# Projection results in ring tiles, two to a tile, with an aligned layout and an earlier split, in a hybrid decoder layer on one core

## The chip, the cores and the metric

The kernel runs on one core of a Trainium2 chip. The metric is device time in microseconds of one execution. TensorE (PE in the profile, with its weight loads as PEld) multiplies, VectorE (DVE) and ScalarE (ACT) do elementwise work and copy results out of PSUM, the queue of SyncE (SP) loads weights and stores results, and the queue of GpSimd (POOL) loads and stores the mixer's data. Each engine takes its instructions in the order in which a scheduler has put them when the program is built.

## The reference

One layer over 2048 rows of width 1024, in float32:

```python
mod = cond @ w_ada + b_ada                      # six vectors: shift, scale, gate, twice
h = modulated_rmsnorm(x, norm_mix, shift1, scale1)
z = h @ w_in                                    # split in 14 pieces
mixed = concatenate([gla_group(...), hgrn2_group(...), mlstm_group(...)])
x = x + gate1 * (mixed @ w_out)
h = modulated_rmsnorm(x, norm_mlp, shift2, scale2)
ff = square(relu(h @ w_ff1)) @ w_ff2            # 1024 -> 4096 -> 1024
x = x + gate2 * ff
return rms(x) * final_norm
```

The three groups are chunkwise linear attentions of different kinds with 64-wide heads. They carry a state along the sequence.

## The kernel before

The sequence is cut in four quarters of 512 rows. A float32 operand of a large matmul is split in a high part (a cast to float32r, on ScalarE, line 193) and a low part (what is left, on VectorE, line 194). Each product is three matmuls: high by high, high by low, low by high.

**Stage 1, the projections** (`inproj`, lines 771 to 878). The four quarters run one after the other. The columns of `w_in` form nine groups, in the order f, q, conv, hout, gout, m, gqk, hi, gv. A group has four row tiles of 128, each in a PSUM bank of its own, and its weights come in four parts (`part`), so the four banks are complete one after the other at the group's end. `evac` then copies each bank out, with the function that the group needs, into a buffer `st`, of which there are three, and stores it to DRAM; a buffer is free when its store has landed. `conv` uses `st` as well, and the two tags `st` and `cvr` also serve the gate step `gla_gate`. The normalized and modulated input of a quarter is eight tiles `ht` of a ring of 15 (`ring`, line 212), a tile being a high and a low half of 512 columns. The tiles of the next quarter are made by `h_k` (lines 224 to 226: VectorE, ScalarE, VectorE), which the program emits in the last group.

**Mixer work in the background.** `mix` and `block_pass` compute the attentions of a quarter from what stage 1 has stored. The program emits their pieces between large matmuls, by `pump`, which keeps a budget against due times; `finish(q)` emits what is left of quarter q. `prog.hold` keeps a new quarter of `mix` from starting while its buffers are lent out.

**Stage 2** per quarter: the output projection (`outproj_in` loads the mixed rows into lent mixer buffers, called spare, and splits them into ring tiles; `outproj` multiplies them and adds x), the norm (`rstd`, with the matmul `ps_ms`) and modulation into h2 (`ffn_in`), and the feed-forward: `f1` makes one tile of 128 hidden columns, `f2` multiplies a block of such tiles and adds into `acc`. A quarter has 32 hidden tiles in six blocks of 5, 6, 6, 6, 5 and 4. The output projections of quarters 1 and 2 stand ahead of the last `f2` of the quarter before. The one of quarter 3 is emitted earlier; its mixed tiles `mt`, its h2 tiles `h` and the weights of the very last block lie in a pool `lp` that takes over the mixer's space on the right-hand side of SBUF.

Within what is emitted, the scheduler orders by priority and readiness: a block under `ahead()` is taken earlier, one under `late()` later, and a tile can only be given out when a buffer of its tag is free.

Of the kernel before, what the change touches and what calls it, by code (L numbers as in the profile page):

```python
# [14 lines left out]
P = 128  # L15
# [86 lines left out]
def trunk(ctx, tc, I, out):  # L102
# [20 lines left out]


    mpx, ipx = ExitStack(), ExitStack()
    mpool = lambda name, bufs: mpx.enter_context(tc.tile_pool(name=name, bufs=bufs, side="right"))
# [70 lines left out]

    def weights(src, n, lp=None):

        with ahead():  # L200
            nraw[0] += 1
            if raw3 and nraw[0] % 3 == 0 and n <= 816:
                raw = raw3[0].tile([P, 816], F32, tag="raw3", name="raw", bufs=1)
            else:
                raw = wp.tile([P, 1024], F32, tag="raw", name="raw", bufs=2)
            r = raw[:, 0:n]
            dma(out=r, in_=src)
            wt = (lp or wp).tile([P, 2, 1024], F32R, tag="wt", name="wt", bufs=4 if lp else 3)
            split(wt[:, 0, 0:n], wt[:, 1, 0:n], r)
        return wt[:, :, 0:n]  # L210

# [93 lines left out]
    SG4 = m1.tile([P, 128], F32, name="SG4")  # L305
    SC = m1.tile([P, 2, 130], F32, name="SC")
    zero = m1.tile([P, 384], mybir.dt.bfloat16, name="zero")
    vaug = m1.tile([P, 4, 65], F32, name="vaug")
    mcar = m1.tile([4, 1], F32, name="mcar")
    Sd = m1.tile([P, 784], F32, name="Sd")  # L310
# [33 lines left out]
    def gates(q):  # L344

        g = gm[q % 3]
        li, y = g[:, 0, :], g[:, 1, :]
        w = lambda n, c=128: m1.tile([P, c], F32, tag="g_" + n, name="g_" + n)
        al, mt, b, be, lf, sm = w("al"), w("mt", 129), w("b"), w("be"), w("lf"), w("sm", 6)
# [40 lines left out]
        for pr in range(2):  # L390
            mm_late(ps[:, 4 * pr:4 * pr + 4], cst[:, 392 + 128 * pr:520 + 128 * pr], sm[:, 2:6], True, True)
        sc = m1.tile([P, 2, 4], F32, tag="sc", name="sc", bufs=2)
        V.tensor_copy(out=sc, in_=ps[:, 0:8].rearrange("p (a c) -> p a c", a=2))
# [32 lines left out]
    def chunk(q, n, L, N):  # L426
# [120 lines left out]
        with hold:  # L547
            for pr in range(2):
                mm_late(psx_[:, pr, 260:390], L.qk[:, pr, :], SC[:, pr, :], True, True)
            for h in range(4):  # L550
                mm_late(psv[:, 65 * h:65 * h + 65], pe[:, h, :], vaug[:, h, :], True, True)
        hi_ = m1.tile([P, 4, 65], F32, tag="hi_", name="hi_")
        V.tensor_tensor(out=hi_.rearrange("p (a h) c -> p a h c", a=2),
# [11 lines left out]
        nxt(load_al)  # L565
        st = m1.tile([P, 56], F32, tag="st40", name="st40")
        den, mu, ss, rs = st[:, 0:4], st[:, 4:8], st[:, 8:24], st[:, 24:40]
# [203 lines left out]
    def inproj(q, hts, nxt):  # L771
# [7 lines left out]
        def conv(ct, src):  # L779
            raw = st_(515, "cvr", 2)  # L780
            V.tensor_copy(out=raw[:, 0:3], in_=hist[:, ct, :])
            A.copy(out=raw[:, 3:515], in_=src)
            V.tensor_copy(out=hist[:, ct, :], in_=raw[:, 512:515])
            y = st_(512)
            cw = lambda t: pc[:, PC_CV + 4 * ct + t:PC_CV + 4 * ct + t + 1]
            A.activation(out=y, in_=raw[:, 0:512], func=AF.Copy, scale=cw(0))
            for t in range(1, 4):
                V.scalar_tensor_tensor(out=y, in0=raw[:, t:t + 512], scalar=cw(t), in1=y,
                                       op0=ALU.mult, op1=ALU.add)
            A.activation(out=raw[:, 0:512], in_=y, func=AF.Sigmoid)  # L790
            V.tensor_tensor(out=y, in0=y, in1=raw[:, 0:512], op=ALU.mult)
            dma_s(out=R.zm[q][ct], in_=y)

        def evac(kind, ti, ps, n):
            r = slice(128 * ti, 128 * ti + 128)
            if kind == "conv":
                return conv(ti, ps)
            s_ = st_(n)
            if kind == "f":
                k_ = st_(n)  # L800
                A.activation(out=s_, in_=ps[:, 0:n], func=AF.Sigmoid)
# [32 lines left out]
        def part(g, c0, n, ps, kk):  # L834

            kind = GROUPS[g][0]
            w = weights(I[f"wg{g}"][:, 2 * kk:2 * kk + 2, c0:c0 + n], 2 * n).rearrange("p a (k n) -> p a k n", k=2)
            for ti in range(len(ps)):
# [89 lines left out]
    def outproj_in(q, lp=None):  # L928
        mt = []
        if lp is None:  # L930
            raws = spare(SPARE_Z, lambda c: R.zx[q][:, c, :])
        for c in range(KT):
            if lp is None:
# [57 lines left out]

    def f1(h2, ft):
        w = weights(I["w1"][ft].rearrange("p c n -> p (c n)"), 1024)
        hd = ring()
        ps = psd.tile([P, 512], F32, tag="psd", name="ps_f1")
        for k in range(KT):
            for i, (a, b) in enumerate(PASSES):
                mm(ps, w[:, b, 128 * k:128 * k + 128], h2[k][:, a], k == 0 and i == 0, k == KT - 1 and i == 2)
            if k % 2:
                pump(1.3)  # L1000
        with ahead():
            r = m5()
# [192 lines left out]
    for q in range(NQ):  # L1195
        hds = []
        for ft in range(NF[0]):
# [6 lines left out]
        for b in range(LB):  # L1204
# [7 lines left out]
            for i in range(1, NF[b + 1]):  # L1212
                nh.append(f1(h2, F0[b + 1] + i))
                next(steps, None)
            hds = nh
            if q == NQ - 2 and b == EARLY:
                finish(NQ - 1)
                mpx.close()
                lp = ctx.enter_context(tc.tile_pool(name="lp", bufs=1, side="right"))
                sm1 = outproj(NQ - 1, outproj_in(NQ - 1, lp), lp)  # L1220
# [4 lines left out]
        if q < NQ - 2:  # L1225
            finish(q + 1)
            h2n = []
            steps = ffn_in(h2n, q + 1, *outproj(q + 1, outproj_in(q + 1)))
        f2(hds, LB, acc, steps)
# [36 lines left out]
```

## Time and profile before

| | us |
|---|---|
| median of 3 runs | 2625.88 (2619.48 to 2629.32) |
| the profiled execution | 2632.36 |
| its span | 2630.3 |
| TensorE busy in it | 2545.6 (97%) |
| VectorE busy | 1787.1 (68%) |
| ScalarE busy | 1232.5 (47%) |

The profile is one execution, so its numbers are set against its own time and not against the median. In a list of waits a row reads: who waited, for whom, microseconds in total, how often, the longest. In a timeline: start, duration, engine, line, operation, tile written and tiles read, count, and in brackets the idle time before it with what ended it. In a group of instructions: count, then busy microseconds and mean nanoseconds of one, then the idle time before them. In a table of windows: the stretch and its length, busy time and count of PE, PEld, DVE, ACT and POOL, then the granted clock of TensorE, the DMA engines' share and GB/s. A large matmul is listed with some 390 ns, though they follow each other every 228 ns (144 in 32.83 us); the length of a long run of equal matmuls tells their pace better than the mean of one.

### The profile page before, as it was taken

The numbers are of one execution on the slowest core, as the hardware profiler recorded it, in microseconds if no ns is written. First come the engines' busy times: TensorE is split into PE (matmuls) and PEld (weight loads), VectorE is DVE, ScalarE is ACT, GpSimd is POOL, SyncE is SP. The second block draws the span as 40 slices with busy tenths as digits, with TensorE's granted clock in tenths as the row PEclk, the third lists the DMA queues.
The fourth block names the chain that finished last, engine by engine and source line by source line (L and its number), as shares of the span: only waits on it lengthen the run. The fifth ranks groups of instructions, "written<-read, shape, count | busy, mean of one in ns | idle before, by whom it ended". The sixth has DMA issues, their size and how long they took to land. (4 is left out here: it accounts for less than half of the span.)

```text
span 2630.3 us, 39618 instructions
## 1 busy us (share of the span) xinstructions
PE 2545.6 (97%) x15050; PEld 2177.5 (83%) x15050; DVE 1787.1 (68%) x3344; ACT 1232.5 (47%) x2191; POOL 259.9 (10%) x435
## 2 busy tenths in 40 slices
PE   5899999999999999999999999999999999999998
PEld 5889888899888788888878888888888888888887
DVE  8785786987975978876887666547566645533335
ACT  4654455545643634554453545445445543433333
POOL 0101102021102112112110000100000010000000
PEclk9999999999999999999999999999999999999999
DMA  8777676586457345446464343444433254433332
GB/s 266 211 222 218 180 216 189 170 243 198 144 143 234 107 113 146 138 142 166 128 184 135 125 131 116 146 133 161 131 123 119 88 181 148 141 114 93 94 96 80
DMA packets 160199, 401.75 MB, mean 153 GB/s; under 512 B 20473, under 2 KB 60490, under 8 KB 160010
## 3 DMA queue, kind: packets, MB, share of 16 engines
q1 hardware_dynamic: 129338, 306.51, 37.3%
q0 software_dynamic: 30672, 92.73, 12.7%
q8 instruction: 118, 1.93, 0.3%
q14 instruction: 71, 0.58, 0.1%
HBM read 336.21 MB, written 62.95 MB: 152 GB/s over the span
## 5 line engine op out<-in xcount | busy, mean ns | idle before, releaser
L165 PE MATMUL ps_f<-ht,wt 128*128 128x512 f32 (+1 forms) x5472 | 1252.3, 388 | 5.6 <-ACT ht L225 5.5
L165 PEld LDWEIGHTS ps_f<-ht,wt 128*128 128x128 f32 x5472 | 1008.8, 188 | 213.4 <-ACT ht L225 6.1
L194 DVE TENSOR_TENSOR wt<-raw,wt 128x1024 fp32r<-128x1024 f32 (+3 forms) x436 | 499.1, 1146 | 431.3 <-ACT wt L193 429.6
L193 ACT CAST wt<-raw 128x1024 fp32r<-128x1024 f32 (+3 forms) x436 | 431.6, 991 | 665.2 <-PE ps_f L165 345.4
L165 PE MATMUL ps_ip<-wt,ht 128*128 128x384 f32 (+2 forms) x3072 | 593.6, 352 | 29.4 <-ACT st L823 8.6
L165 PEld LDWEIGHTS ps_ip<-wt,ht 128*128 128x128 f32 x3072 | 554.6, 193 | 56.2 <-ACT st L823 10.6
L1023 DVE SCALAR_TENSOR_TENSOR acc<-ps_f,mod,acc 128x512 f32<-128x512 f32 (+1 forms) x200 | 145.1, 727 | 106.0 <-PE ps_f L165 105.3
L1003 ACT ACTIVATE m<-ps_f 128x512 f32<-128x512 f32 x128 | 76.9, 601 | 288.4 <-PE ps_f L165 288.2
L165 PE MATMUL ps_f<-h,wt 128*128 128x512 f32 x768 | 181.4, 397 | 0.0
L165 PEld LDWEIGHTS ps_f<-h,wt 128*128 128x128 f32 x768 | 144.6, 188 | 35.6 <-issue 0.5
L165 PE MATMUL ps_op<-ht,wt 128*128 128x512 f32 x576 | 133.1, 393 | 3.8 <-ACT ht L193 3.8
L165 PEld LDWEIGHTS ps_op<-ht,wt 128*128 128x128 f32 x576 | 109.0, 190 | 26.9 <-ACT ht L193 3.9
L323 POOL DMA_DIRECT2D blk<-zq x144 | 93.6, 661 | 353.0 <-DVE prod L333 169.4
L333 DVE TENSOR_TENSOR prod<-blk 128x768 f32<-128x768 f32 (+3 forms) x192 | 111.1, 578 | 2.6
L334 DVE TENSOR_REDUCE Sd<-prod 128x48 f32<-128x768 f32 (+3 forms) x192 | 110.5, 576 | 2.9
L1006 DVE TENSOR_TENSOR ht<-m,ht 128x512 fp32r<-128x512 f32 x128 | 88.2, 689 | 22.3 <-ACT m L1005 22.2
L332 DVE TENSOR_TENSOR blk<-blk 128x720 f32<-128x720 f32 (+4 forms) x180 | 98.9, 550 | 1.6 <-DMA blk<-zq 1.4
L165 PE MATMUL ps_ip<-ht,wt 128*128 128x512 f32 x384 | 100.0, 410 | 0.0
L165 PEld LDWEIGHTS ps_ip<-ht,wt 128*128 128x128 f32 x384 | 73.2, 196 | 15.6 <-issue 1.4
L1005 ACT ACTIVATE m<-m 128x512 f32<-128x512 f32 x128 | 81.1, 634 | 2.8
L1004 ACT ACTIVATE ht<-m 128x512 fp32r<-128x512 f32 x128 | 81.3, 635 | 0.1
L189 ACT ACT_TABLE_LOAD x57 | 73.1, 1283 | 1.0
(390 smaller groups left out, 2355.7 us busy)
## 6 DMA issues: line engine op xcount, KB each, us to landing
raw<-w SPq DMA_DIRECT2D x256, 512.0 KB, 3.5
raw<-wg SPq DMA_DIRECT2D x100, 384.0 KB, 4.0
m<-wada SPq DMA_DIRECT2D x64, 256.0 KB, 3.9
raw<-wo SPq DMA_DIRECT2D x32, 512.0 KB, 3.6
m<-xq SPq DMA_DIRECT2D x56, 256.0 KB, 3.5
raw<-wg SPq DMA_DIRECT2D x28, 512.0 KB, 5.0
blk<-zq POOLq DMA_DIRECT2D x144, 96.0 KB, 6.7
zt<-zq POOLq DMA_DIRECT2D x48, 288.0 KB, 4.4
```

Of the source, the lines that this page charges most:

```text
L165: T.matmul(out=ps, lhsT=l, rhs=r, start=start, stop=stop)
L193: A.copy(out=hi, in_=src)
L194: V.tensor_tensor(out=lo, in0=src, in1=hi.bitcast(F32), op=ALU.subtract)
L323: dma_m(out=t[i][32 * g:32 * g + 32], in_=src)
L332: V.tensor_tensor(out=t[1][:, 0:n, :], in0=t[1][:, 0:n, :], in1=t[2][:, d:16, :], op=ALU.mult)
L333: V.tensor_tensor(out=prod[:, 0:n, :], in0=t[1][:, 0:n, :], in1=t[0][:, d:16, :], op=ALU.mult)
L334: V.tensor_reduce(out=s49[:, 0:n, d:d + 33:16], in_=prod[:, 0:n, :].rearrange("p j (u c) -> p j u c", c=16), op=ALU.add, axis=AX.X)
L1003: A.activation(out=r, in_=ps, func=AF.Relu)
L1004: A.activation(out=hd[:, 0], in_=r, func=AF.Square)
L1005: A.activation(out=r, in_=r, func=AF.Square)
L1006: V.tensor_tensor(out=hd[:, 1], in0=r, in1=hd[:, 0].bitcast(F32), op=ALU.subtract)
L1023: V.scalar_tensor_tensor(out=acc[:, dt, c], in0=ps, scalar=mod[:, 40 + dt:41 + dt], in1=acc[:, dt, c], op0=ALU.mult, op1=ALU.add)
```

## The change

Four things are edited.

1. Results of the projections go into ring tiles. `pair()` takes a ring tile as two float32 halves of 512 columns; a result uses the first, and group f, which stores two results of a row tile, both. `conv` takes its tile there too. The group gv of quarters 0 to 2 keeps `st`.
2. Weights of a projection part are laid out with each of the two input tiles on a multiple of 128 columns. This moves only group q, with 408 columns.
3. Buffers on the right-hand side are padded to multiples of 64 bytes, and the side begins with a small tile `top`; a tile `gap` does the same for `lp`. The tiles there, before at 32 bytes past a multiple of 64, start on the multiple.
4. For quarters 1 and 2, `finish` and `outproj_in` are emitted within the last `f1` tile ahead of the output projection, behind that tile's matmuls, and `prog.hold` is set there.

```diff
@@ right-hand pools, alignment
+    ctx.enter_context(tc.tile_pool(name="top", bufs=1, side="right")).tile([P, 8], F32, name="top")
...
-    SC = m1.tile([P, 2, 130], F32, name="SC")
+    SC = m1.tile([P, 272], F32, name="SC")[:, 0:260].rearrange("p (a c) -> p a c", a=2)
-    vaug = m1.tile([P, 4, 65], F32, name="vaug")
-    mcar = m1.tile([4, 1], F32, name="mcar")
+    vaug = m1.tile([P, 272], F32, name="vaug")[:, 0:260].rearrange("p (h c) -> p h c", h=4)
+    mcar = m1.tile([4, 16], F32, name="mcar")[:, 0:1]
...
-        w = lambda n, c=128: m1.tile([P, c], F32, tag="g_" + n, name="g_" + n)
+        w = lambda n, c=128: m1.tile([P, (c + 15) // 16 * 16], F32, tag="g_" + n, name="g_" + n)[:, 0:c]
...
                 mpx.close()
+                ctx.enter_context(tc.tile_pool(name="gap", bufs=1, side="right")).tile([P, 32], F32, name="gap")
                 lp = ctx.enter_context(tc.tile_pool(name="lp", bufs=1, side="right"))
@@ weights
-    def weights(src, n, lp=None):
+    def weights(src, n, lp=None, ks=1):
...
-            split(wt[:, 0, 0:n], wt[:, 1, 0:n], r)
-        return wt[:, :, 0:n]
+            if ks == 1:
+                split(wt[:, 0, 0:n], wt[:, 1, 0:n], r)
+                return wt[:, :, 0:n]
+            m = n // ks
+            wv = wt[:, :, 0:ks * ((m + 127) // 128 * 128)].rearrange("p a (k s) -> p a k s", k=ks)[:, :, :, 0:m]
+            split(wv[:, 0], wv[:, 1], r.rearrange("p (k s) -> p k s", k=ks))
+        return wv
@@ inproj
-            y = st_(512)
+            y = pair()[0]
...
+        def pair():
+
+            t = ring().bitcast(F32)
+            return t[:, 0], t[:, 1]
+
         def evac(kind, ti, ps, n):
...
-            s_ = st_(n)
+            if kind == "gv" and q < NQ - 1:
+                s_ = st_(n)
+            else:
+                s_, k_ = (t[:, 0:n] for t in pair())
             if kind == "f":
-                k_ = st_(n)
...
-            w = weights(I[f"wg{g}"][:, 2 * kk:2 * kk + 2, c0:c0 + n], 2 * n).rearrange("p a (k n) -> p a k n", k=2)
+            w = weights(I[f"wg{g}"][:, 2 * kk:2 * kk + 2, c0:c0 + n], 2 * n, ks=2)
@@ outproj_in, f1
             raws = spare(SPARE_Z, lambda c: R.zx[q][:, c, :])
+        prog.hold = lp is None and q > 0
...
-    def f1(h2, ft):
+    def f1(h2, ft, before=None):
+
         w = weights(I["w1"][ft].rearrange("p c n -> p (c n)"), 1024)
...
+        if before:
+            before()
         with ahead():
             r = m5()
@@ main loop
-        hds = []
+        hds, mts = [], []
...
             for i in range(1, NF[b + 1]):
-                nh.append(f1(h2, F0[b + 1] + i))
+                early = q < NQ - 2 and b == LB - 1 and i == NF[LB] - 1
+                if early:
+                    finish(q + 1)
+                    prog.hold = True
+                nh.append(f1(h2, F0[b + 1] + i, (lambda: mts.extend(outproj_in(q + 1))) if early else None))
...
         if q < NQ - 2:
-            finish(q + 1)
             h2n = []
-            steps = ffn_in(h2n, q + 1, *outproj(q + 1, outproj_in(q + 1)))
+            steps = ffn_in(h2n, q + 1, *outproj(q + 1, mts))
```

The scheduler moves instructions nearly everywhere. Three places follow, as the program lists them; equal neighbours stand in one row, and line numbers are those of the kernel listed, so lines 193, 225, 823 and 1003 to 1005 are 195, 233, 838 and 1022 to 1024 in the changed one.

On ScalarE, from quarter 1 to quarter 2, before. `ht<-m,mod` is a modulated tile of the next quarter; line 818 is a copy out of group m, three groups ahead of the last:

```order
L225 ACTIVATE ht<-m_5628,mod 128x512
L225 ACTIVATE ht<-m_5634,mod 128x512
L225 ACTIVATE ht<-m_5695,mod 128x512
L225 ACTIVATE ht<-m_5701,mod 128x512
L193 CAST wt<-raw 128x768
L818 ACT_TABLE_LOAD
L818 ACTIVATE st<-ps_ip 128x256
```

The same engine and modulated tiles now; line 838 with x4 copies out group hi, the last but one:

```order
L195 CAST wt<-raw 128x768 x2
L838 COPY ht<-ps_ip 128x384 x4
L195 CAST wt<-raw 128x768
L233 ACTIVATE ht<-m_5561,mod 128x512
L233 ACTIVATE ht<-m_5567,mod 128x512
L233 ACTIVATE ht<-m_5620,mod 128x512
L233 ACTIVATE ht<-m_5626,mod 128x512
L654 ACTIVATE sq<-ps_oo 128x384
L195 CAST wt<-raw 128x768
```

All eight modulations now stand between the copies out of hi and those of gv; before, two more stood ahead of the four shown, one behind the copies of m, and one in the last group.

On ScalarE at the last `f1` tile ahead of quarter 1's output projection, before. `m<-ps_f` is the Relu of an `f1` result, `ht<-spare` a cast of a mixed tile:

```order
L1003 ACTIVATE m_11840<-ps_f_11809 128x512
L193 CAST wt<-raw 128x1024
L1004 ACTIVATE ht<-m_11840 128x512
L193 CAST ht<-spare 128x512
L1005 ACTIVATE m_11840<-m_11840 128x512
L193 CAST ht<-spare 128x512 x7
```

Now, with ps_f_11797 the result of that last tile:

```order
L195 CAST ht<-spare 128x512
L1024 ACTIVATE m_11786<-m_11786 128x512
L195 CAST ht<-spare 128x512 x5
L1022 ACTIVATE m_11863<-ps_f_11797 128x512
L195 CAST ht<-spare 128x512 x2
L1023 ACTIVATE ht<-m_11863 128x512
L195 CAST wt<-raw 128x1024
L1024 ACTIVATE m_11863<-m_11863 128x512
```

Six of the eight casts have moved ahead of the last result's Relu. On TensorE the gate transposes `ps_g`, which stood just ahead of this output projection, now stand one `f2` tile behind it.

On TensorE at the output projection of quarter 0, before (`ps_g`, `ps_sc` and `ps_t` are the mixer's next transposes and a small product, `ps_ms` the norm's matmul):

```order
L165 MATMUL ps_ip<-wt,ht 128x384 x226
L165 MATMUL ps_op<-ht,wt 128x512 x192
L184 MATMUL ps_g<-cst,g_be 128x128
L184 MATMUL ps_g<-cst,g_al 128x128
L184 MATMUL ps_g<-cst,g_b 128x128
L184 MATMUL ps_g<-cst,g_lf 128x128
L180 MATMUL ps_sc<-g_sm,cst 128x4 x2
L184 MATMUL ps_t<-cst,zt 128x128 x15
L165 MATMUL ps_ms<-sm,cst 128x512
```

Now:

```order
L167 MATMUL ps_ip<-wt,ht 128x384 x228
L186 MATMUL ps_g<-cst,g_be 128x128
L186 MATMUL ps_g<-cst,g_al 128x128
L186 MATMUL ps_g<-cst,g_b 128x128
L186 MATMUL ps_g<-cst,g_lf 128x128
L182 MATMUL ps_sc<-g_sm,cst 128x4 x2
L186 MATMUL ps_t<-cst,zt 128x128 x2
L167 MATMUL ps_op<-ht,wt 128x512 x192
L186 MATMUL ps_t<-cst,zt 128x128 x13
L167 MATMUL ps_ms<-sm,cst 128x512
```

The transposes moved ahead of the output projection. On ScalarE its eight casts, before spread over the groups hi and gv, stand in one row behind the last copy out of gv.

More of the change, by code (lines that the diff above doesn't have):

```diff
@@ L391, in gates @@
             mm_late(ps[:, 4 * pr:4 * pr + 4], cst[:, 392 + 128 * pr:520 + 128 * pr], sm[:, 2:6], True, True)
-        sc = m1.tile([P, 2, 4], F32, tag="sc", name="sc", bufs=2)
+        sc = m1.tile([P, 16], F32, tag="sc", name="sc", bufs=2)[:, 0:8].rearrange("p (a c) -> p a c", a=2)
         V.tensor_copy(out=sc, in_=ps[:, 0:8].rearrange("p (a c) -> p a c", a=2))
@@ L551, in chunk @@
                 mm_late(psv[:, 65 * h:65 * h + 65], pe[:, h, :], vaug[:, h, :], True, True)
-        hi_ = m1.tile([P, 4, 65], F32, tag="hi_", name="hi_")
+        hi_ = m1.tile([P, 272], F32, tag="hi_", name="hi_")[:, 0:260].rearrange("p (h c) -> p h c", h=4)
         V.tensor_tensor(out=hi_.rearrange("p (a h) c -> p a h c", a=2),
@@ L565, in chunk @@
         nxt(load_al)
-        st = m1.tile([P, 56], F32, tag="st40", name="st40")
+        st = m1.tile([P, 64], F32, tag="st40", name="st40")
         den, mu, ss, rs = st[:, 0:4], st[:, 4:8], st[:, 8:24], st[:, 24:40]
```

## The prediction

> **What bounds the kernel now.** I read the page's head first, then the windows by stage (TensorE busy, VectorE busy, granted clock), then the lists of waits of TensorE and ScalarE, and last the timelines at the places that the change touches.
>
> ```profile
> span 2630.3 us, 39618 instructions
> PE 2545.6 (97%) x15050; PEld 2177.5 (83%) x15050; DVE 1787.1 (68%) x3344; ACT 1232.5 (47%) x2191; POOL 259.9 (10%) x435
> ...
> 0.00:215.00 215.00, 175.26 (x870) 160.49 (x871) 168.22 (x332) 113.42 (x177) 26.14 (x50) 0.96 0.77 233
> 215.00:408.00 193.00, 189.38 (x991) 176.23 (x990) 139.18 (x238) 87.65 (x139) 21.06 (x33) 0.97 0.70 202
> 408.00:615.00 207.00, 200.67 (x1458) 183.86 (x1456) 170.14 (x367) 113.02 (x232) 27.10 (x45) 1.00 0.69 205
> 615.00:829.00 214.00, 203.67 (x1425) 188.19 (x1424) 158.44 (x344) 107.35 (x214) 34.64 (x56) 0.96 0.57 169
> 829.00:2630.00 1801.00, 1776.65 (x10313) 1468.77 (x10312) 1151.15 (x2064) 811.01 (x1432) 150.91 (x252) 1.00 0.42 130
> ```
>
> The first four windows are the input projections of quarters 0 to 3, the fifth is everything behind them; the columns are stretch, length, then busy time and count of PE, PEld, DVE, ACT and POOL, granted clock, DMA share, GB/s. TensorE bounds the kernel in every stage. So a change pays only through TensorE: fewer idle gaps, less time at a low clock, or matmuls that follow each other faster. The idle time sits in the projections (40, 4, 6 and 10 us); behind them it is 24 us of 1801.
>
> ```profile
> PE ps_ip L165 <- ACT st L823: 8.6, 6, 4.4
> PE ps_ip L165 <- ACT cvr L782: 4.0, 2, 3.6
> PE ps_gt L883 <- DVE st L810: 3.9, 3, 2.9
> PE ps_ip L165 <- DVE st L777: 2.6, 2, 1.9
> PE ps_ip L165 <- ACT st L815: 2.3, 1, 2.3
> PE ps_ip L165 <- ACT st L802: 1.6, 3, 1.0
> PE ps_ip L165 <- ACT st L819: 1.3, 2, 1.0
> ...
> PE ps_op L165 <- ACT ht L193: 3.8, 2, 1.9
> ...
> ACT st L823 <- DMA zv<-st: 17.7, 7, 7.5
> ACT st L801 <- DMA zq<-st: 5.2, 3, 2.5
> ACT st L814 <- DMA zq<-st: 3.7, 2, 2.4
> ACT st L776 <- DMA zg<-st: 3.6, 2, 2.6
> ```
>
> Each row gives total, count and longest. The first seven, 24.3 us, are TensorE waiting until a projection result has left its PSUM bank. The last four show why the copies out are late: ScalarE waits until the store of an earlier `st` buffer has landed, because there are three of them for groups of four results. The `ps_op` row belongs to the early split.
>
> **The change, part by part.**
>
> *Results in ring tiles.* Where both waits meet looks like this, ScalarE first, then TensorE, then the clock in the six microseconds behind:
>
> ```profile
> 811.89 0.48 ACT L823 COPY st<-ps_ip 128x384 f32<-128x384 f32 x1 [7.52 <-DMA zv<-st]
> 812.42 16.33 PE L165 MATMUL ps_ip<-wt,ht 128*128 128x384 f32 x78 [4.40 <-ACT st L823]
> ...
> 812.00:818.00 6.00, 5.58 (x18) 5.58 (x18) 2.61 (x3) 2.55 (x4) 1.64 (x3) 0.50 0.75 192
> ```
>
> With seven ring tiles beside the eight that hold h, four results never wait for their own stores, so such a wait goes. What stays: `cvr` and `gn` still share two buffers (much of L782), and a transpose of gate columns still needs its result (L810). The bounds are 0 and 24.3 us; I take six tenths, 15 us, since the last four rows name stores as the cause for the very lines (L823, L802, L776/777, L814/815) that hold most of it. The last group of quarters 0 to 2 keeps `st`, and nothing else but the gate step uses it then, so at most its fourth result waits. A long wait also costs clock: here the row behind shows 0.50. Its price comes from the next fence: 192 identical matmuls took 45.45 us behind a wait that lowered the clock, 43.89 us behind one that did not, so 1.5 us. Five of the waits above were 1.9 us or longer; I count three restarts saved, 4.5 us (bounds 0 and 7.5).
>
> *Early split.* For quarters 1 and 2 the output projection starts with a wait of 1.88 us for the first cast of `spare`, which ScalarE can only issue behind the last FFN-1 result:
>
> ```profile
> 1274.17 45.45 PE L165 MATMUL ps_op<-ht,wt 128*128 128x512 f32 x192 [1.88 <-ACT ht L193]
> ...
> 1736.90 43.89 PE L165 MATMUL ps_op<-ht,wt 128*128 128x512 f32 x192 [1.88 <-ACT ht L193]
> ...
> 1274.00:1278.00 4.00, 3.83 (x11) 3.03 (x12) 4.00 (x8) 4.00 (x9) 0.00 (x0) 0.67 0.40 131
> ```
>
> In the new order six casts stand ahead of that result, fed by three free ring tiles and by h2 tiles that the last FFN-1 tile releases one by one. What is queued behind them on ScalarE is only that result's own Relu, with a whole output projection ahead of its use. Both waits go: 3.8 us, plus the one restart of 1.5, is 5.3 us (bounds 0 and 5.3). The gate transposes that stood there move a few rows later; they cost TensorE the same.
>
> By the Trainium skill, "TensorE: Matmul & The Clock Gate", Part 1, the clock falls only after an idle window of about 3.4 us. Then only the waits of 3.6 and 4.4 us would be charged and the sum below would be about 3 us smaller. The 0.67 behind a wait of 1.88 us disagrees, and I go by the row.
>
> *Layout.* As allocated in the two programs, tiles of the right-hand pools move from 32 bytes past a multiple of 64 to the multiple itself. Matmuls that stream such tiles can be compared with the same matmul on `ht` tiles, which already start on a multiple:
>
> ```profile
> 2144.45 45.14 PE L165 MATMUL ps_op<-mt,wt 128*128 128x512 f32 x192
> ...
> 2323.07 33.89 PE L165 MATMUL ps_f<-h,wt 128*128 128x512 f32 x144
> 2356.80 32.83 PE L165 MATMUL ps_f<-ht,wt 128*128 128x512 f32 x144
> ...
> L165 PE MATMUL ps_f<-h,wt 128*128 128x512 f32 x768 | 181.4, 397 | 0.0
> ```
>
> 144 matmuls on `h` take 1.06 us longer than 144 on `ht`, and there are 768 of them in quarter 3: 5.65 us. The 192 on `mt` took 45.14 against 43.89 for `ht`: 1.25 us. Together 6.9 us, with 0 as the other bound if it is not the address. The 408-column weights and the mixer's small matmuls I count at nothing, their rows being too mixed to tell.
>
> *What it costs.* First, the modulated tiles of the next quarter. Before, `ht` tiles for them were free two or three groups ahead; now results hold those tiles, and all eight modulations fall into the last group. Each is two VectorE instructions and one of ScalarE:
>
> ```profile
> L226 DVE SCALAR_TENSOR_TENSOR ht<-m,mod,ht 128x512 fp32r<-128x512 f32 x24 | 17.8, 747 | 4.5 <-ACT ht L225 4.4
> L224 DVE SCALAR_TENSOR_TENSOR m<-m,A,rs 128x512 f32<-128x512 f32 x24 | 16.9, 746 | 0.1
> L225 ACT ACTIVATE ht<-m,mod 128x512 fp32r<-128x512 f32 x24 | 16.9, 737 | 11.7 <-DVE m L224 10.6 <-PE ps_ip L165 0.9
> ...
> 212.00:229.00 17.00, 17.00 (x100) 17.00 (x99) 4.48 (x5) 5.64 (x9) 3.81 (x6) 1.00 0.98 260
> 390.00:407.00 17.00, 17.00 (x99) 17.00 (x99) 10.05 (x23) 5.86 (x10) 7.90 (x13) 1.00 0.82 216
> 590.00:612.00 22.00, 22.00 (x149) 21.83 (x148) 15.72 (x33) 12.13 (x31) 5.88 (x10) 1.00 0.79 225
> ```
>
> The windows are the last groups of quarters 0, 1 and 2. Eight times 1.49 us is 11.9 us more VectorE work in each: 16.4 of 17 us, 21.9 of 17, 27.6 of 22. The cover is the VectorE time freed in the groups ahead and the weight splits that run up to two buffers ahead; what is late next is a weight split queued behind the modulations, for which TensorE waits. If none of the excess is covered it is 4.9 + 5.6 us and two restarts, 13.5 us; if all is, nothing. I take 4 us, nearer to covered, because mixer work in those windows can slide.
>
> Second, the output projection of quarter 0: before, its casts were spread over the last two groups; now all eight stand behind the last result, and TensorE does the gate transposes meanwhile, which used to fill a bubble that stays:
>
> ```profile
> 872.16 0.27 PE L184 MATMUL ps_g<-cst,g_be 128*128 128x128 f32 x1
> ...
> 873.63 1.86 PE L184 MATMUL ps_t<-cst,zt 128*128 128x128 f32 x15 [0.54 <-DVE gT L387]
> ...
> 883.23 64.70 PE L165 MATMUL ps_f<-ht,wt 128*128 128x512 f32 x276 [5.48 <-ACT ht L225]
> ...
> L193 ACT CAST ht<-spare 128x512 fp32r<-128x512 f32 x24 | 13.6, 618 | 5.3 <-DMA spare<-zx 4.3 <-PE ps_ip L165 0.7
> ```
>
> From the first gate transpose to `ps_t`, 872.16 to 873.63, are 1.5 us, which leave the time in which TensorE waits for the norm anyway (5.48 us). They cover ScalarE's first two casts of 0.62 us; one wait of about 0.3 us is left for the rest: 1.8 us (bounds 0 and 6.5, eight casts in full and a restart). Third, the transposes of gate columns stand nearer behind their results in group q: 1.5 us (bounds 0 and 3.9, all that L810 costs now).
>
> Sum: 15 + 4.5 + 5.3 + 6.9 - 4 - 1.8 - 1.5 = 24.4 us less. The profiled execution took 2632.4 us (span 2630.3 and 2.1 around it) and would take 2608.0; it lies 6.5 us above the median of the runs, so the median goes from 2625.9 to 2601.5.
>
> **Rivals.** *VectorE piles up (slower).* The modulations of the next quarter in the last group of quarters 0 to 2 hide behind nothing: 11.9 us and a restart, 13.4 us at each of three places, 40.2 in place of 4. That is 11.8 us slower, 2637.7. It decides from 9.5 us a place, where the gain of 28.4 is used up. For it: two windows over their length. Against it: 139 of 193 us VectorE in the whole quarter.
>
> *The waits change name.* The copies out leave early, but TensorE then waits for weight splits at the same places; nothing of the 19.5 us comes. 2621.0. For it: VectorE at 158 to 170 us of 207 to 215. Against it: hardly any wait of TensorE for a weight split stands in the list now.
>
> *The address is not the cause.* The 6.9 us stay: 2608.4. Against it: `h` and `mt` lie far apart and pay alike. The Trainium skill, "SBUF — State Buffer", Door 1, gives 16-byte lines as the grain of reads; 32 past 64 is a multiple of 16, so by it the move changes nothing. The slower rows on `h` and `mt` speak against that so far.
>
> *The early split does not start early*, since the casts wait for h2 tiles until the output projection begins: 2606.8.
>
> **How the numbers follow.** My forecast 0.52, waits change name 0.18, address 0.13, VectorE 0.10, no early start 0.07. A difference below 0.5%, 13 us, cannot be told from none here. Faster by more (below 2612.8): nine tenths of the forecast, most of the address and early-split cases, a fifth of the second case: 0.68. Slower (above 2639): half of the VectorE case, 0.05, and 0.03 for stalls at places that I don't see: 0.08. Within: 0.24. The forecast's own range is 2590 to 2611; to leave out no more than 0.2, with bounds of the waits taken in, it is 2586 to 2622.
>
> **What would show it.** Right: ScalarE's waits for stores all but gone outside the last group of quarters 0 to 2, TensorE's seven rows down to about 9 us in total; `ps_op` of quarters 1 and 2 without a wait; 144 matmuls on `h` in 32.8 us. Wrong: windows of the last groups with TensorE below its length and a wait for `wt` L194 or `ht` L225 (its new line); an unchanged 33.9 us on `h`; a wait of several microseconds ahead of the first `ps_op`. The forecast falls if TensorE's idle time in the four projections stays near 60 us.

## The result and the profile after

| | before | after |
|---|---|---|
| median of the runs, us | 2627.60 (2619.48 to 2633.78, 6 runs) | 2610.41 (2607.28 to 2612.68, 6 runs) |
| ratio, 95% interval | | 0.9933 (0.9914 to 0.9953) |
| span of the profiled execution, us | 2630.3 | 2609.7 |
| TensorE busy in it, us | 2545.6 | 2529.5 |

The change makes the kernel 17.2 us faster by the medians. The forecast was 2601.5 us; the measured time is 8.9 us above it, in the range and on the side that was forecast. The terms are another matter, and most of this part is about them.

First the windows by stage of the kernel after (quarters 0 to 3 of the projections, each from its first projection matmul to that of the next quarter, then everything behind them; columns as before):

```profile
0.00:219.00 219.00, 180.76 (x928) 168.04 (x929) 164.12 (x324) 107.19 (x171) 28.08 (x53) 0.97 0.74 222
219.00:394.30 175.30, 168.55 (x904) 157.36 (x902) 133.60 (x232) 79.14 (x129) 21.52 (x34) 1.00 0.68 206
394.30:608.70 214.40, 207.56 (x1470) 191.45 (x1470) 181.08 (x384) 122.11 (x237) 23.02 (x39) 0.98 0.63 194
608.70:818.60 209.90, 203.85 (x1451) 188.69 (x1448) 156.75 (x340) 104.07 (x217) 35.64 (x57) 0.98 0.65 203
818.60:2609.70 1791.10, 1768.77 (x10305) 1467.98 (x10304) 1150.43 (x2068) 813.92 (x1438) 151.34 (x253) 1.00 0.42 130
```

The projections end at 818.6 in place of 828.6 us. TensorE's idle time in them is 818.6 - 760.7 = 57.9 us; before, the first four windows left 60.0. So of the ten microseconds that this one execution is shorter there, only two are idle time. Some five more are clock: in the projections the trace of before has 13 stretches of 3.41 us in which the granted clock is half, that of after 10, and each costs some 1.7 us (the last section shows such a stretch). What remains of the waits says why so little idle time went (TensorE's list, then ScalarE's, in the projections):

```profile
PE ps_ip L167 <- ACT cvr L790: 7.1, 3, 6.6
PE ps_ip L167 <- ACT st L838: 4.2, 2, 2.5
PE ps_gt L898 <- DVE ht L825: 3.1, 2, 1.8
PE ps_ada L167 <- DVE sm L287: 2.4, 2, 1.2
PE ps_ip L167 <- DVE wt L196: 2.3, 1, 2.3
PE ps_ip L167 <- ACT ht L817: 2.1, 1, 2.1
PE ps_ip L167 <- ACT ht L834: 0.2, 1, 0.2
...
PE ps_ip L167 <- DVE sm L260: 3.8, 3, 1.7
PE ps_ada L167 <- DVE td L629: 0.8, 1, 0.8
...
ACT cvr L790 <- DMA zq<-gn: 6.7, 1, 6.7
ACT st L838 <- DMA zv<-st: 6.4, 3, 3.9
```

The copies out (`cvr`, `st`, `ht`) account for 7.1 + 4.2 + 3.1 + 2.1 + 0.2 = 16.7 us, where the seven rows of before had 24.3 and about 9 were expected. Of these 7.6 us, 5.4 come back in other waits, most of them for VectorE's norm, `ada` and mixer work: the rows `sm` L260, `sm` L287 and `td` hold 3.8 + 2.4 + 0.8 = 7.0 us, where before had one row of 1.9:

```profile
PE ps_ip L165 <- DVE sm L252: 1.9, 2, 1.5
```

The same rows hold 0.8 to 2.0 us in the six kernels of this document with the results in `st`, and 3.7 to 8.4 us in the eight with results in ring tiles. So they come with the ring tiles; what in VectorE's order makes them was not tested.

The largest wait for a copy, 6.6 us, is a single one: the first copy of the convolution group of quarter 0 needs a `cvr` buffer, and `gn` of the gate step, which uses the same two buffers, has not been stored yet. The same place, ScalarE, before (first row, from the kernel before) and after:

```profile
114.61 0.59 ACT L782 COPY cvr<-ps_ip 128x512 f32<-128x512 f32 x1 [3.48 <-DMA zq<-gn]
```
```profile
114.76 0.58 ACT L790 COPY cvr<-ps_ip 128x512 f32<-128x512 f32 x1 [6.69 <-DMA zq<-gn]
...
115.00:121.00 6.00, 5.60 (x19) 5.61 (x20) 5.42 (x12) 3.24 (x5) 0.00 (x0) 0.54 0.35 103
```

The copy starts at the same time in both, 114.6 and 114.8 us. In the kernel after the engines are there three microseconds earlier and wait three microseconds longer: what was gained ahead of this point is given back at it, and the clock behind it is 0.54.

Behind the projections the two small parts did what the prediction said:

```profile
1265.16 43.68 PE L167 MATMUL ps_op<-ht,wt 128*128 128x512 f32 x192
...
1723.39 43.68 PE L167 MATMUL ps_op<-ht,wt 128*128 128x512 f32 x192
...
2131.18 43.68 PE L167 MATMUL ps_op<-mt,wt 128*128 128x512 f32 x192
...
2307.27 32.80 PE L167 MATMUL ps_f<-h,wt 128*128 128x512 f32 x144
...
L167 PE MATMUL ps_f<-h,wt 128*128 128x512 f32 x768 | 175.7, 390 | 0.0
```

`ps_op` of quarters 1 and 2 has no wait ahead of it and takes 43.68 us (45.45 and 43.89 before). 144 matmuls on `h` take 32.80 us (33.89), the 768 together 175.7 (181.4), and `ps_op` on `mt` 43.68 (45.14).

At the output projection of quarter 0 something is lost, TensorE first, then VectorE:

```profile
862.26 1.58 PE L186 MATMUL ps_t<-cst,zt 128*128 128x128 f32 x13
867.88 1.93 PE L167 MATMUL ps_ms<-sm,cst 128*128 128x512 f32 x2 [4.04 <-DVE sm L242]
...
876.16 2.07 PE L167 MATMUL ps_f<-ht,wt 128*128 128x512 f32 x4 [4.76 <-ACT ht L233]
...
863.20 0.48 DVE L369 TENSOR_TENSOR_SCAN g_mt<-g_lf,g_mt,gm 4x128 f32<-4x128 f32 x1
...
864.98 0.74 DVE L983 SCALAR_TENSOR_TENSOR acc<-ps_op,mod,acc 128x512 f32<-128x512 f32 x1
```

`ps_op` ends at 862.4 us, but VectorE takes its result 2.6 us later (0.4 us before), since gate scans and block work of the mixer stand ahead of it in its order. From there to the first FFN matmul the kernel takes 13.7 us; before, 10.9.

**How the runs are read below.** Behind the first `ps_op` matmul, what two kernels share nearly repeats from profile to profile: most stretches within 0.1 us, an output projection within the 1.6 us of one clock restart, and the whole rest of `weights_pad` and of the kernel before within 0.1 us. What varies there is the clock: the traces have 7 to 17 us of half clock in this part, which makes up to 5 us of time. In the projections more than that varies. `early_only` below has the projections of the kernel before, and its profile shows 797.5 us for them against 802.8. So for each kernel I take the time from the first `ps_op` to the end from its trace, and what is left of the median of its runs, less 2.0 us around the span, is its time up to there, "projections" for short. The kernel before with 23 runs (2626.87) gives 823.1, `early_only` 821.5; layout alone 817.5, layout with early split, which has the same projections, 819.5. Such numbers are good to about 2 us, and to about 5 where the trace has most half clock behind the first `ps_op` (17 us in `ring_only` and `gv_st_all`). Each ratio is to the kernel before in the same series of runs, where its median was 2625.8 to 2627.6.

| kernel | median, us | ratio to before, 95% | projections | rest |
|---|---|---|---|---|
| before | 2626.87 | | 823.1 | 1801.7 |
| layout_only | 2613.40 | 0.9947 (0.9935 to 0.9960) | 817.5 | 1793.9 |
| early_only | 2621.52 | 0.9973 (0.9959 to 0.9987) | 821.5 | 1798.1 |
| ring_only | 2625.26 | 0.9996 (0.9985 to 1.0008) | 817.7 | 1805.6 |
| no_ring | 2610.58 | 0.9943 (0.9929 to 0.9956) | 819.5 | 1789.1 |
| after | 2610.41 | 0.9933 (0.9914 to 0.9953) | 817.3 | 1791.1 |
| weights_pad | 2627.93 | 1.0005 (0.9991 to 1.0019) | 824.3 | 1801.7 |
| gate_ring | 2600.76 | 0.9899 (0.9884 to 0.9914) | 807.7 | 1791.0 |
| gate_only | 2604.99 | 0.9916 (0.9897 to 0.9935) | 811.1 | 1791.9 |
| pack | 2604.88 | 0.9915 (0.9900 to 0.9930) | 812.4 | 1790.5 |
| hi_gv_st | 2623.86 | 0.9989 (0.9979 to 0.9999) | 831.5 | 1790.4 |
| gv_st_all | 2611.69 | 0.9942 (0.9927 to 0.9956) | 813.0 | 1796.7 |
| pack_gate | 2600.49 | 0.9901 (0.9882 to 0.9920) | 808.5 | 1790.0 |
| pack_gate_gv | 2601.21 | 0.9903 (0.9886 to 0.9920) | 807.7 | 1791.5 |

### The profile page after: what moved, and what is told of

It is laid out like the page before. It is cut to its first block, busy times and chain, and to the rows that moved or that the text cites. A ratio compares the mean times of both kernels' runs of the same rounds, so it can differ in the third digit from the quotient of the medians.

```text
span 2609.7 us, 39539 instructions
## 1 busy us (share of the span) xinstructions
PE 2529.5 (97%) x15050; PEld 2173.5 (83%) x15050; DVE 1786.0 (68%) x3344; ACT 1226.4 (47%) x2190; POOL 259.6 (10%) x435
## 3 DMA queue, kind: packets, MB, share of 16 engines
q0 software_dynamic: 30672, 92.73, 12.2%
## 5 line engine op out<-in xcount | busy, mean ns | idle before, releaser
L167 PE MATMUL ps_f<-h,wt 128*128 128x512 f32 x768 | 175.7, 390 | 0.0
```

The source lines that it names most:

```text
L167: T.matmul(out=ps, lhsT=l, rhs=r, start=start, stop=stop)
```

## The experiments

### The three parts alone

**layout_only**: the kernel before with `top`, `gap`, the rounded widths and the spread weights of the change, nothing else.

```diff
+    ctx.enter_context(tc.tile_pool(name="top", bufs=1, side="right")).tile([P, 8], F32, name="top")
...
-            w = weights(I[f"wg{g}"][...], 2 * n).rearrange("p a (k n) -> p a k n", k=2)
+            w = weights(I[f"wg{g}"][...], 2 * n, ks=2)
```

> The kernel before with only the layout part of the change. If the address of the streamed tile is what made the matmuls on `h` and `mt` slower, `ps_f<-h,wt` falls from 397 ns to about 390 ns each and `ps_op<-mt,wt` x192 from 45.1 to 43.7 us: 6.5 to 7.5 us less in all, everything in quarter 3, nothing in the four projections. If something else that differs between the two programs made them faster (the order of the instructions, the clock), the rows keep 397 ns and 45.1 us and the time stays within 2 us of before.

Measured: 13.5 us faster. Its rows in quarter 3 are those of the whole change:

```profile
2132.82 43.68 PE L167 MATMUL ps_op<-mt,wt 128*128 128x512 f32 x192
```

Together with the matmuls on `h` (three stretches of quarter 3 shorter by 0.55, 2.84 and 2.50 us) that is 7.35 us, without ring tiles or early split. So the place of the tiles, and not the order of the work, makes these matmuls faster. The 6.9 us of the forecast were right for quarter 3. Another 5.6 us lie in the projections, where none were expected.

**weights_pad** asks where those come from: the kernel before with only the spread weights.

```diff
-    def weights(src, n, lp=None):
+    def weights(src, n, lp=None, ks=1):
...
+            w = weights(I[f"wg{g}"][...], 2 * n, ks=2)
```

> The kernel before with only the second half of each projection weight tile moved to the next multiple of 128 columns (of the layout part, the piece that touches the projections' 408-column weights alone). The 384 matmuls of 408 columns fell from 356 to 350 ns with the layout part, which is 2.1 us: if that is all that the piece does, it is 1 to 3 us faster than the kernel before. The layout part alone was 13.5 us faster, of which only 7.3 us lie in quarter 3: if the rest comes from the weights of the projections, it is 5 to 7 us faster; if it comes from the right-hand tiles that the mixer and the loads use, only 1 to 3.

Measured: no difference that the runs can tell, and its 408-column row is that of before; the fall from 356 to 350 ns in layout_only was not the weights' doing:

```profile
L165 PE MATMUL ps_ip<-wt,ht 128*128 128x408 f32 x384 | 76.8, 356 | 1.8 <-ACT st L808 1.3 <-DVE wt L194 0.5
```

The mean of a row that mixes full and half clock is too coarse for this piece. Back to back at full clock, matmuls on the second half of these weights follow each other in 186.8 to 187.5 ns in the three traces with the old place (before, early_only, ring_only), and in 184.9 to 185.8 in the eleven with the new one; those on the first half, which did not move, take 184.7 to 185.1 everywhere. That is some 2 ns for 192 matmuls, 0.4 us.

So the 5.6 us belong to the right-hand tiles, if they are not in part scatter (the other kernel with the same projections, no_ring, has 3.6). What can be seen there is that some loads into these tiles land sooner. Of the lists of transfers in the first 800 us, first the kernel before, then layout_only (KB each, median us from issue to landing):

```profile
blk<-zq POOLq DMA_DIRECT2D x75, 96.0 KB, 6.8
mqk_t<-zm POOLq DMA_DIRECT2D x5, 256.0 KB, 5.3
```
```profile
blk<-zq POOLq DMA_DIRECT2D x84, 96.0 KB, 6.5
mqk_t<-zm POOLq DMA_DIRECT2D x5, 256.0 KB, 4.7
```

The three kernels with the old places and results in `st` (before, early_only, weights_pad) have 6.8, 6.9, 6.9 and 5.3, 6.1, 6.0 in these two rows, the three with the new places and results in `st` (layout_only, no_ring, gate_only) 6.5, 6.1, 6.1 and 4.7, 4.9, 4.6. But `ring_only`, with the old places, has 6.0 and 5.1, and the whole change, with the new ones, 5.9 and 5.3, so the rows do not go by the place alone. What shortens the projections here stays open.

**early_only**: the kernel before with only the fourth part of the change.

```diff
+                early = q < NQ - 2 and b == LB - 1 and i == NF[LB] - 1
+                if early:
+                    finish(q + 1)
+                    prog.hold = True
+                nh.append(f1(h2, F0[b + 1] + i, (lambda: mts.extend(outproj_in(q + 1))) if early else None))
```

> The kernel before with only the early split. If the two waits of 1.88 us ahead of `ps_op` of quarters 1 and 2 and the slow stretch behind one of them are the gain, it is 5 to 7 us faster and both `ps_op` groups take about 43.7 us without a wait. If in the whole change the gain at these places came from the results in ring tiles or the layout, it is within 2 us of before.

Measured: 5.35 us faster. Both waits are gone:

```profile
1266.90 43.68 PE L165 MATMUL ps_op<-ht,wt 128*128 128x512 f32 x192
...
1726.90 43.68 PE L165 MATMUL ps_op<-ht,wt 128*128 128x512 f32 x192
```

Ahead of each `ps_op` 2.8 us are gone, the wait and the gate transposes, which TensorE now does behind it; the first `ps_op` is 1.77 us shorter, the second 0.21. Of two equal waits of 1.88 us only one had cost clock, as the forecast had counted. In all, the trace is 3.6 us shorter behind the first `ps_op`. The other 1.7 us of the medians lie in projections that are the same in both kernels, so they are scatter.

**ring_only**: the kernel before with only the first part.

```diff
-            y = st_(512)
+            y = pair()[0]
...
-            s_ = st_(n)
+            if kind == "gv" and q < NQ - 1:
+                s_ = st_(n)
+            else:
+                s_, k_ = (t[:, 0:n] for t in pair())
```

> The kernel before with only the input projection results in ring tiles. The forecast gave this part 15 + 4.5 - 4 - 1.8 - 1.5 = 12.2 us less. The comparison of the two traces gives 11.7 us less in the projections and 2.8 us more at the output projection of quarter 0, so about 9 us less. If the waits only change their name, it is within 3 us of before. What the forecast of the whole change was short of (20.6 us less between the profiled executions, 24.4 expected) should show here: fewer than 12 us.

Measured: 1.6 us faster by the medians, an interval that includes no change. Its waits of TensorE in the projections:

```profile
PE ps_ip L165 <- ACT cvr L782: 7.1, 2, 6.9
PE ps_ip L165 <- ACT ht L225: 6.0, 4, 1.7
PE ps_ip L165 <- ACT st L830: 5.5, 2, 3.5
PE ps_ip L165 <- ACT ht L809: 4.9, 3, 3.2
PE ps_ip L165 <- DVE sm L252: 3.7, 3, 1.6
```

Against the seven rows of before, `st` L823 (8.6, now L830) fell by 3.1, while `cvr` rose by 3.1 and L802 (now L809) by 3.3. The projections are 5.4 us shorter, and 3.8 us are lost behind them, 2.9 of them in the bubble ahead of the first FFN matmul. TensorE's idle time in the projections of the profiled execution is no smaller, 61 us against 60; the half clock is, 10 stretches against 13. So the waits did change their name: some 6 us went into waits for other copies and stores (`cvr`, `ht` L809), and some 6 into waits for VectorE (`sm`, `ada` and `td` 6.7 in place of 1.9, weight splits 2.3 in place of 0.9).

**no_ring**: layout and early split together.

```diff
-            s_, k_ = (t[:, 0:n] for t in pair())
+            s_ = st_(n)
```

> Layout and early split together, without the results in ring tiles. If the three parts add up, it is the sum of the two single parts, 12 to 14 us faster than before, and about 6 to 9 us slower than the whole change. If the parts help or hinder each other (the ring tiles are used by both the early split and the results), the difference from the sum is over 3 us.

Measured: 2610.58, as fast as the whole change. The ring tiles, the largest part of the diff and of the forecast, add 0.2 us to the other two, which cannot be told from nothing (the intervals of both ratios overlap). The single gains, 13.5 + 5.35 + 1.6 = 20.4, do not add up to the 16.5 of the whole against the same 2626.87: the 5.4 and 5.6 us of ring tiles and layout in the projections become 5.8 together.

### Where the gain of the ring tiles goes

**gate_ring**: the whole change, with the gate step's tiles in ring tiles as well.

```diff
-        ga = [ipool.tile([P, 2, 192], F32, tag="st", name="ga", bufs=3) for _ in range(2)]
-        gn = [ipool.tile([P, 2, 192], F32, tag="cvr", name="gn", bufs=2) for _ in range(2)]
+        gt_ = [ring().bitcast(F32)[:, :, 0:384].rearrange("p b (a c) -> p b a c", a=2) for _ in range(2)]
+        ga, gn = [t[:, 0] for t in gt_], [t[:, 1] for t in gt_]
```

> The whole change, and the two tiles of the gate step (`ga` and `gn`) go into the halves of ring tiles too, so that `cvr` is left to the convolution alone. If the removed waits came back because `cvr` still waits for the store of `gn` (6.6 us of TensorE at about 115 us, 7.1 us in all, where the kernel before had 4.0), the row of TensorE waiting for `cvr` falls to about 1 us and the time by 6 to 8 us, to 2602 to 2605. If this wait only hides another one behind it (the weight splits, the modulations), the row goes and the time stays within 3 us of the 2610.4 of the whole change.

Measured: 2600.76, 9.7 us less than the whole change and 26.1 less than before. The row is gone, nothing of its size takes its place:

```profile
PE ps_ip L167 <- ACT ht L817: 3.6, 2, 2.3
PE ps_ip L167 <- ACT st L838: 3.2, 2, 2.3
PE ps_ip L167 <- ACT cvr L790: 0.2, 1, 0.2
```

The 6.9 us of the row and some 2.8 of slow clock behind it (0.54 for six microseconds above) are the size of the 9.6 us in the projections. The two profiled executions differ there by more, 15.5 us: idle time by 7.8, and the stretches at half clock, 4 against 10, by some 10. This execution was the fastest of its kernel.

**gate_only**: the same gate tiles, but all results on `st` and `cvr`.

```diff
-                s_, k_ = (t[:, 0:n] for t in pair())
+                s_ = st_(n)
...
+        ga, gn = [t[:, 0] for t in gt_], [t[:, 1] for t in gt_]
```

> Layout and early split as in the whole change, the projection results on the `st` and `cvr` buffers as in the kernel before, and only the two tiles of the gate step (`ga`, `gn`) in ring tiles: one step of the change left out, one added. It is the missing corner of a square: neither results nor gate tiles in the ring 2610.6 us, results alone (the whole change) 2610.4, both 2600.8. If the 9.6 us of the gate tiles come from the one wait for `gn` and its slow clock alone, they come here too: 2601 to 2603, and the results in ring tiles are needless. If results and gate tiles hinder each other on `st` and `cvr` as well, and only moving both frees them, this stays at 2606 to 2612, and then the results in ring tiles are worth 5 to 11 us, hidden in the whole change behind the wait for `gn`.

Measured: 2604.99, between the two theories. The square is now full:

| | gate tiles on `st`, `cvr` | gate tiles in the ring |
|---|---|---|
| results on `st`, `cvr` | 2610.58 | 2604.99 |
| results in the ring | 2610.41 | 2600.76 |

Results in the ring are worth 0.2 us as long as the gate tiles block `cvr`, and 4.2 us when they do not. The two kernels of the right column scatter by 7 and 11 us over 5 and 6 runs and their intervals overlap, so the 4.2 is likely but not certain; the 5.6 us of the gate tiles alone are clear of it. Taken as measured, the wait for `gn` hid about four microseconds. Even so it is a third of the 12.2 us that the forecast gave this part net.

**hi_gv_st**: a second group back on `st`.

```diff
-            if kind == "gv" and q < NQ - 1:
+            if kind in ("hi", "gv") and q < NQ - 1:
```

> The whole change, but in quarters 0 to 2 the group ahead of the last keeps the `st` buffers as well, so that ring tiles are free for the modulations one group earlier. If the ring is short there: starts of quarters 1 to 3 without waits, but some 2 us per quarter of waits for `zv<-st` stores come back (the eight stores of two groups go through three buffers), in sum 0 to 6 us less than the whole change. If the ring is not short, 3 to 8 us more, since only the old waits come back.

Measured: 13.5 us slower than the whole change, more than either expectation; the old waits are back (11.6 us for `st`, in the whole change 4.2), and a new one is there. What is saved in quarter 3 (the row of `ada` for `sm`, 2.4 us in the whole change) is less than that:

```profile
PE ps_ip L167 <- ACT st L838: 11.6, 5, 4.9
PE ps_gt L898 <- DVE ht L825: 6.7, 3, 2.8
PE ps_ada L167 <- DVE td L629: 5.3, 1, 5.3
```

Ring tiles freed in this way do not pay for the stores of eight successive results through three buffers.

**pack**: two successive results to a ring tile.

```diff
+        half = []
+
+        def one():
+            if not half:
+                half.extend(pair()[::-1])
+            return half.pop()
```

> The whole change, but two successive results share one ring tile (in the change itself every result except that of group f takes a tile of its own and leaves the other half empty). Half as many ring tiles are held. If the modulated tiles of the next quarter come late because results hold the ring, TensorE's waits at the starts of quarters 1 to 3 (`ht` L233 and the `ada` matmuls, about 3 us each) go: 4 to 8 us less than the 2610.4 of the whole change. If the ring is not what is short, within 2 us of it.

Measured: 2604.88, 5.5 us less. The wait for `cvr` is still there (7.3 us), while `sm`, `ada` and `td` hold 3.7 us in place of 7.0; whether that is the gain is open. By the expectation this speaks for a ring that is short, hi_gv_st against it; **pack_gate**, pack with the gate tiles in the ring, decides.

```diff
-                s_, k_ = (t[:, 0:n] for t in pair())
+                s_ = one()[:, 0:n]
...
+        ga, gn = [t[:, 0] for t in gt_], [t[:, 1] for t in gt_]
```

> The whole change with both additions, two successive results to a ring tile (alone 2604.9 us) and the gate tiles in ring tiles (alone 2600.8). If they remove different waits, the gains of 5.5 and 9.6 us add up: 2594 to 2597. If both reach the same bound (VectorE and ScalarE in the last group and the starts of the quarters), it stays at 2599 to 2602.

Measured: 2600.49, the same as gate_ring. With `cvr` free, half as many ring tiles in use bring nothing. **pack_gate_gv** puts the last group of quarters 0 to 2 into ring tiles too.

```diff
-            if kind == "gv" and q < NQ - 1:
+            if False:
```

> As the last one, and the last group of quarters 0 to 2 goes into ring tiles as well, two results to a tile. The waits of TensorE for the copies of that group (4.2 us in the whole change, with the stores `zv<-st` as the cause) go: 3 to 6 us less than with both additions alone. If the modulated tiles of the next quarter are then held up by these results, the waits for `ht` L233 at the starts of quarters 1 to 3 grow by 2 us or more each and it is the same or slower.

Measured: 2601.21, again the same. Its wait for the copies of that group is gone, and one of 4.6 us for the copies of group m has come:

```profile
PE ps_ip L167 <- ACT ht L826: 4.6, 1, 4.6
```

Three kernels end at 2600.5 to 2601.2, about 26 us faster than before and 10 us faster than the change. gate_ring is the smallest edit among them.

**gv_st_all** tests the loss ahead of the first FFN matmul: the last group on `st` in quarter 3 as well.

```diff
-            if kind == "gv" and q < NQ - 1:
+            if kind == "gv":
```

> The whole change, but the last group keeps `st` in quarter 3 as well. If the 2.8 us that the whole change loses between the end of the output projection of quarter 0 and the first FFN matmul come from the ring tiles that the last results hold, they come back there (10.9 us instead of 13.7), and the wait of about 4 us for the store ahead of the last result at about 810 us comes back in their place, with 1.5 us of slow clock behind it: within 4 us of the whole change. If the loss has another cause, it stays at 13.7 us and the whole is 4 to 6 us slower.

Measured: the loss is larger, 17.0 us from the last `ps_op` to the first `ps_f` (13.7 in the whole change, 10.9 before), the total the same within 1.3 us. Ring tiles held by the last results are not its cause. gate_only, with all results on `st`, has 13.2. There the matmul ahead ends at 849.7 us and VectorE is late in the same way:

```profile
849.92 0.40 DVE L342 TENSOR_REDUCE Sd<-prod 128x15 f32<-128x240 f32 x1
850.24 0.35 DVE L340 TENSOR_TENSOR blk<-blk 128x192 f32<-128x192 f32 x1
...
851.28 0.74 DVE L976 SCALAR_TENSOR_TENSOR acc<-ps_op,mod,acc 128x512 f32<-128x512 f32 x1
```

An earlier end of the projections is not the cause: layout_only ends them at 817.4 us, earlier than the whole change, and keeps 10.9. What the late kernels share is other mixer work in VectorE's order around the last result. An order without that work at this place was not tested.

## Why the prediction was right, and where it was wrong

*The number and its direction* came out, the forecast 2601.5, the measurement 2610.4; the range of 2586 to 2622 holds it. Two errors of opposite sign helped, so that the total came this near is partly luck.

*Results in ring tiles, 15 us: the step that failed.* The prediction took six tenths of the 24.3 us in seven rows. They fell by 7.6 us, and other waits took 5.4 back. Alone this part gave 5.4 us in the projections and 1.6 in all; on top of the other parts 0.2. The sentence "What stays: `cvr` and `gn` still share two buffers (much of L782)" was right, but it treated that wait as a fixed 4.0 us. A wait with a fixed end grows by what is saved ahead of it, and it did, to 7.1 (gate_ring and gate_only show it). The prediction's own test, idle time staying near 60 us, applies: it is 57.9. The rival "the waits change name" is the better account of this part, except that weight splits (2.3 us in one row) were the smallest part of what they changed to: the wait for `gn` and VectorE's `sm`, `ada` and `td` were more.

*Three clock restarts, 4.5 us.* The size is near: three stretches of half clock fewer, some 5 us. That results in ring tiles save them is not shown, since layout_only, without those, has 10 stretches as well.

*The modulations, 4 us, and the gate transposes, 1.5 us.* The pile-up did not happen as forecast: with `cvr` free, fewer ring tiles in use (pack_gate) gain nothing, and no wait for modulated tiles was added (`ht` L233 has 6.0 us in the kernels on both sides, all in quarter 0). VectorE was late all the same, at other places: the 5.1 us that `sm`, `ada` and `td` grew by are the size of the term, but not its path. The transposes cost 3.1 in place of 3.9 us, 0.8 less where 1.5 more was forecast.

*The output projection of quarter 0, 1.8 us.* The size was near, 2.8 us, the mechanism wrong: TensorE does not wait for the casts of the mixed rows, `ps_op` begins at once; VectorE is late at the last result.

*Early split, 5.3 us.* Right in its parts, the two waits and one restart of 1.8 us at their places. The sum is smaller: 3.6 us in the trace behind the first `ps_op`, and 5.35 by medians that carry scatter of the projections.

*Layout, 6.9 us.* Right in quarter 3, 7.35 us. It missed the 4 to 6 us in the projections that the same part brings alone. Those are the second error, and part of them is the same time that the ring tiles would have saved.

The rival "the address is not the cause" falls, and with it, for these matmuls, the rule that 16 bytes are the grain of reads, which the prediction weighed from the Trainium skill, "SBUF — State Buffer", Door 1: 0 instead of 32 bytes past a multiple of 64 took the row on `h` from 397 to 390 ns with nothing else changed that its matmuls touch. The rivals "VectorE piles up" and "the early split does not start early" fall with the rows above.

## What to carry to other kernels

Before a wait is counted as gained, look along the same engine for the next wait whose end does not move with it, a store that must land or a shared buffer; the saving stops there, and that buffer is the one to free first (here two gate tiles, 9.7 us, while moving all results was worth 0.2). An edit with several parts should be timed part by part: here the smallest-looking one, some padding, brought most. Where a stage scatters by more than the effect between executions and the rest nearly repeats, take the rest from the trace and the stage from the medians, and set the granted clock of each run beside its time.

## What was not expected of the hardware

Streaming from tiles at 32 bytes past a multiple of 64 costs: 33.89 against 32.80 us for 144 matmuls of 512 columns, 7.6 ns each. The price is not the same for every operand: the second half of the 408-column weights lay 1632 bytes into its tile, which is also 32 past a multiple of 64, and there the matmuls followed each other only some 2 ns slower than at 2048. What makes the difference between the two is open.

The granted clock of these traces is 1.00 or 0.50 and nothing between; a value such as 0.67 is the mean of a window. Within an execution the half-clock stretches lie on a grid of 3.41 us, and whether one comes goes by how busy TensorE was in the stretch before it. In the fourteen traces, all 62 full-clock stretches of that grid with TensorE busy for less than 0.43 of the time were followed by half clock, 19 of 51 with 0.43 to 0.55, and 19 of some 10,200 with more. The two equal waits of 1.88 us of the kernel before are an example, two windows on the grid for each:

```profile
1271.90:1275.35 3.45, 1.57 (x10) 1.28 (x9) 3.45 (x8) 3.45 (x7) 0.00 (x0) 1.00 0.02 8
1275.35:1278.75 3.40, 3.40 (x10) 2.61 (x9) 3.40 (x7) 3.38 (x8) 0.00 (x0) 0.50 0.47 154
...
1732.75:1736.15 3.40, 2.27 (x15) 1.89 (x13) 1.32 (x6) 1.88 (x3) 0.00 (x0) 1.00 0.44 146
1736.15:1739.55 3.40, 2.65 (x11) 2.04 (x12) 3.40 (x6) 3.40 (x8) 0.00 (x0) 1.00 0.33 107
```

The first wait lies in one stretch (TensorE busy 1.57 of 3.45 us), and the next runs at half clock. The second falls on the border of two (2.27 and 2.65 of 3.40 us) and costs no clock.

The scatter between executions goes with this clock. Of 56 runs of the kernel before, the two at a granted clock of 0.986 took 2633.7 us on average and the four at 0.992 took 2619.4; six thousandths of the span are 15.8 us, and the times differ by 14.3. The scatter is smaller in the kernels with the new layout: the runs of before, early_only, ring_only and weights_pad (12 to 23 in a series) spread over 13 to 18 us, the 11 of hi_gv_st over 6.6, and the 5 or 6 of each other one over 4 to 11, though so few runs spread less by their number too. Why the layout would do this was not tested.
